# Hybrid RG-LRU and band-attention layer: x four steps apart, a PSUM bank for bounds, score slots and accumulators, late v places, gate columns, background counts

## The chip, the cores and the metric

The kernel runs on one core of one Trainium2 chip. The metric is the device time of one execution in microseconds. The engines are TensorE (PE, matmuls, with its weight loads as PEld), VectorE (DVE), ScalarE (ACT), GpSimd (POOL) and SyncE (SP), which only starts transfers. Each takes its instructions in order. PSUM, into which PE writes, has eight banks of 512 fp32 columns; DVE and ACT read it.

## What is computed

One layer of a streaming encoder, for a prompt of 2048 rows and a sample of 32 rows, width 1024, all in fp32:

```python
def layer_front(x, norm_g, w_in, q_g, k_g):
    z = rms_norm(x, norm_g) @ w_in
    xl, gl, q, k, v, ga = jnp.split(z, SPLITS, axis=-1)
    q = rms_norm(q.reshape(B, T, N_HEADS, HEAD_DIM), q_g)
    k = rms_norm(k.reshape(B, T, N_HEADS, HEAD_DIM), k_g)
...
xc, cbuf = causal_conv(xl, zeros, conv_w[l], conv_b[l])          # width 4
lru, h_last = rg_lru(xc, zeros, gate_a_w[l], gate_a_b[l], ...)   # scan over positions
att = band_attention_prompt(q, k, v, rel_bias[l])                # own 64-frame chunk and 8 before
...
def layer_back(x, lru, gl, att, ga, w_out, p, ple_g, w_pg, w_pe):
    mix = jnp.concatenate([lru * jax.nn.silu(gl), att * jax.nn.silu(ga)], axis=-1) @ w_out
    h = x + mix
    gate = jax.nn.sigmoid(rms_norm(h, ple_g) @ w_pg)
    return h + (p @ w_pe) * gate
```

It also returns the last 512 rows of k and v, the last convolution inputs and the LRU state. There are 8 heads of 64; the sample attends to 512 cached keys and its own 32.

## The kernel before

**Numbers.** PE multiplies fp16. Every fp32 operand is split into a high and a low fp16 half after scaling by a power of two from an absolute maximum; `products` issues three matmuls (hi·hi, hi·lo, lo·hi) for each 128 rows of the contraction. The split is `split`: the high half on POOL, ACT or DVE, the low half on DVE (L163). A maximum is spread over the partitions by `all_max`: DVE puts it on a diagonal (dg, L87), PE multiplies it by ones (psm, L90), DVE takes the maximum of the row (L91).

**Tiles.** The prompt is 16 tiles of 128 rows; a pair of tiles is a chunk (`c`, 8 of them) for the LRU. `load_x` and `prep_x` bring in a tile and normalise it: ACT's Square (L223), POOL's and DVE's split, and a transposing DMA into `xT[c][:, i % 2]`. x and xn have one buffer each, xT two (two chunks). `proj(i, b)` makes one of four blocks of 512 columns (1 k, 0 q, 2 v, 3 attention gate) of tile i in 24 matmuls (psp), and the `post_` functions finish it and store it in DRAM. `l_proj` makes the two LRU blocks in groups of 128 columns (psx, 48 matmuls of 256), `l_gates` the block-diagonal gates (psg at L641, read by ACT's sigmoids at L644 and L645), `l_tail` the scan, `l_halves` its halves.

**Order.** No planner: the generators `l_steps` (LRU of a chunk) and `background` (splitting w_out, w_ple_gate, w_ple_proj, the cache, and the bias rows into DRAM) are advanced by a few steps after each `proj` of the main loop, eight steps n = 0 to 7 per chunk. A scheduler then places the instructions on the engines' queues. `x_pair` says in which step of a chunk x is loaded and prepared. After the last chunk the late projections (v of tiles 12 to 15 and the attention gate) follow, without the pool of the early buffers.

**Attention.** A unit is one head of a tile (in tile 1 two heads): `u_scores` (pss, 10 matmuls into 640 columns in two banks), DVE adds the bias and takes the maximum (L988, for mx), ACT the exponential, `u_split` the halves and a transposing DMA (PT), `u_pv` five units later the product with v (pso, one bank for the 8 heads of a tile; `a_out` reads it at L1068 into att). Between the units `fill` advances the output side of the tile before: `o_out` (psu) and `o_gate` (psg and pse, from hT). At the end `fill` runs the sample's output among the last tile's: `prev` is tile 15's gate.

**PSUM before.** Projections: ps_p 3 banks, ps_x 3, ps_g 2 (gates and psm share them). Attention: ps_s two slots of two banks, ps_o 1, ps 3.

## Time and profile before

| what | us |
|---|---|
| median of three runs | 1235.5 (1233.63 to 1238.19) |
| the profiled execution | 1231.86 |
| its span | 1229.9 |
| PE busy in the span | 1078.4 (88%) |
| DVE busy | 850.8 (69%) |
| ACT busy | 591.3 (48%) |
| POOL busy | 430.5 (35%) |

The span is that of the profiled execution, from its first to its last instruction. Busy time says how long an engine worked, not that it was the one the others waited for. The stages lie one behind the other: start-up to 125 us, projections to about 650, the first units of attention to 725, steady attention to 1150, the tail.

### The profile page before, as it was taken

The page shows a single profiled execution, that of the slowest core. Times are in us where ns is not written, and L with a number is a line of the kernel's source. Part 1 is how long each engine was busy: PE and PEld are TensorE (multiplying, and loading weights), DVE is VectorE, ACT ScalarE, POOL GpSimd, SP SyncE. Part 2 cuts the span into 40 slices and gives each one's busy share as a digit, 9 for nine tenths or more (in the row PEclk, how much of TensorE's full clock was granted, in tenths as well). Part 3 has the DMA queues.
Part 4 walks back from the last instruction along what each step waited for, and adds up shares of the span by engine and source line. Part 5 has one row for each costly group of instructions (what it writes and reads, how often), then busy time and mean ns, then how long its engine had stood idle before and what let it go on. Part 6 is the DMA issues. An engine that isn't in the chain of part 4 may idle for free. (4 is left out here: it accounts for less than half of the span.)

```text
span 1229.9 us, 22389 instructions
## 1 busy us (share of the span) xinstructions
PE 1078.4 (88%) x8395; PEld 626.2 (51%) x8395; DVE 850.8 (69%) x1932; ACT 591.3 (48%) x1040; POOL 430.5 (35%) x482
## 2 busy tenths in 40 slices
PE   3779997997697988788988699999999999999896
PEld 1335664653364654565644355555555555555443
DVE  5997557666885676877855676677777777677544
ACT  6542374544636746247654344444445444545223
POOL 3875123444542437452421222222222222222221
PEclk9789998998898998899899699999999999999998
DMA  8785225994856476540498987999989998998841
GB/s 288 212 216 159 75 67 143 263 253 127 228 159 172 143 204 180 167 107 22 146 338 262 239 156 162 171 207 194 191 186 198 181 196 190 185 200 188 187 84 26
DMA packets 357725, 217.47 MB, mean 177 GB/s; under 512 B 296032, under 2 KB 298632, under 8 KB 357488
## 3 DMA queue, kind: packets, MB, share of 16 engines
q1 hardware_dynamic: 357184, 215.50, 72.0%
q8 instruction: 65, 1.06, 0.4%
q10 hardware_dynamic: 432, 0.54, 0.1%
q14 instruction: 44, 0.36, 0.1%
HBM read 98.87 MB, written 46.76 MB: 118 GB/s over the span
## 5 line engine op out<-in xcount | busy, mean ns | idle before, releaser
L183 PE MATMUL psp<-wA,xT 128*128 128x512 f16 x1536 | 368.3, 400 | 30.1 <-ACT sq L656 9.9
L183 PEld LDWEIGHTS <-xT 128*128 128x128 f16 x1536 | 155.9, 102 | 264.2 <-issue 82.0
L994 ACT ACTIVATE S<-S,nb,s 128x640 f32<-128x640 f32 (+5 forms) x130 | 110.5, 850 | 221.4 <-DVE nb L991 211.8
L183 PE MATMUL psg<-g,hT 128*128 128x512 f16 (+1 forms) x792 | 179.8, 376 | 4.4 <-DMA hT<-hn 2.7
L587 PE MATMUL psx<-xT,wl 128*128 128x256 f16 x1536 | 178.7, 276 | 0.0
L587 PEld LDWEIGHTS <-wl 128*128 128x128 f16 x1728 | 157.3, 99 | 25.6 <-issue 2.1
L1010 DVE TENSOR_TENSOR Phl<-S,Phl 128x640 f16<-128x640 f32 (+4 forms) x126 | 96.9, 773 | 89.4 <-POOL Phl L1007 52.7
L1032 PE MATMUL pso<-kv,PT 128*128 128x64 f16 (+1 forms) x1704 | 116.9, 195 | 25.6 <-DMA PT<-Phl 13.2
L1032 PEld LDWEIGHTS <-PT 128*128 128x128 f16 (+2 forms) x1800 | 109.7, 99 | 47.5 <-issue 16.8
L1007 POOL TENSOR_SCALAR Phl<-S 128x640 f16<-128x640 f32 (+4 forms) x63 | 49.1, 779 | 213.7 <-ACT S L994 179.8
L183 PEld LDWEIGHTS <-hT 128*128 128x128 f16 x792 | 73.6, 98 | 79.8 <-DMA hT<-hn 3.4
L977 PE MATMUL pss<-kv,qT 128*128 128x128 f16 (+2 forms) x1200 | 107.0, 221 | 6.3 <-DVE mx L988 4.4
L977 PEld LDWEIGHTS <-qT 128*128 128x128 f16 (+1 forms) x1200 | 93.9, 99 | 19.6 <-issue 6.2
L988 DVE CUSTOM_DVE_ANT_0 S<-pss,bias 128x640 f32<-128x640 f32 (+4 forms) x128 | 93.0, 731 | 2.5 <-PE pss L977 2.0
L183 PE MATMUL psu<-o,AT 128*128 128x512 f16 x384 | 91.8, 390 | 1.3 <-DMA AT<-An 1.3
L183 PE MATMUL psu<-o,L 128*128 128x512 f16 x384 | 88.0, 379 | 0.0
L1148 POOL TENSOR_TENSOR gt<-gt,h 128x512 f32<-128x512 f32 (+1 forms) x32 | 41.7, 1304 | 60.7 <-DVE gt L1147 56.4
L95 POOL TENSOR_SCALAR fh<-ssqh,e 128x8 f32<-128x8 f32 (+1 forms) x34 | 17.5, 514 | 126.4 <-DVE ssqh L282 99.8
L96 POOL TENSOR_TENSOR fh<-fh,pw 128x8 f32<-128x8 f32 (+1 forms) x34 | 61.0, 1793 | 1.6
L183 PEld LDWEIGHTS <-AT 128*128 128x128 f16 x384 | 36.6, 101 | 43.5 <-issue 5.7
L183 PEld LDWEIGHTS <-L 128*128 128x128 f16 x384 | 35.6, 98 | 38.5
L90 PE MATMUL psm<-dg,ones 128*128 128x128 bf16 x25 | 6.0, 241 | 55.7 <-DVE dg L87 29.7
(284 smaller groups left out, 1693.5 us busy)
## 6 DMA issues: line engine op xcount, KB each, us to landing
stw<-in_w_in_dram SPq DMA_DIRECT2D x20, 512.0 KB, 7.1
x<-in_x_prompt_dram SPq DMA_DIRECT2D x16, 512.0 KB, 4.8
stg<-in_w_out_dram SPq DMA_DIRECT2D x16, 512.0 KB, 5.1
stg<-in_w_ple_gate_dram SPq DMA_DIRECT2D x16, 512.0 KB, 4.8
qT<-qd SPq DMA_DIRECT2D x32, 256.0 KB, 5.4
kv<-kvd SPq DMA_DIRECT2D x16, 512.0 KB, 4.1
h<-in_x_prompt_dram SPq DMA_DIRECT2D x16, 512.0 KB, 4.5
out_dram<-gt SPq DMA_DIRECT2D x31, 256.0 KB, 2.3
```

The lines of the kernel that those rows point to most:

```text
L90: nc.tensor.matmul(ps, lhsT=ones, rhs=dg, start=True, stop=True)
L95: nc.gpsimd.tensor_scalar(dst, ssq, mul, add, op0=OP.mult, op1=OP.add)
L96: nc.gpsimd.tensor_tensor(dst, dst, pw[:R, :n], op=OP.pow)
L183: m = nc.tensor.matmul(ps[:R], lhsT=l(a), rhs=r(e), start=first and j == 0, stop=last and j == 2)
L587: m = nc.tensor.matmul(o, lhsT=wl[j][:, k, a, g * 128:(g + 1) * 128], rhs=rhs, start=i == 0, stop=i == 23)
L977: last_mm[0] = nc.tensor.matmul(ps[rw, c], lhsT=q[:, h % 2, a * 4 + h // 2, :R], rhs=k[:, h, :n], start=a == 0, stop=a == 1)
L988: nc.vector.tensor_tensor_reduce(out=S[:, c0:c0 + W], in0=ps[:, c0:c0 + W], in1=bias[:, h, 640 - W:], op0=OP.add, op1=OP.max, scale=1.0, s ...
L994: nc.scalar.activation(S[:, c0:c0 + W], S[:, c0:c0 + W], AF.Exp, bias=nb[:, j:j + 1], scale=scP, accum_out=sums[i][:, e:e + 1])
L1007: nc.gpsimd.tensor_scalar(v[:, 0, :W], P[:, :W], 1.0, 1.0, op0=OP.mult, op1=OP.mult)
L1010: nc.vector.tensor_tensor(v[:, 1, :W], P[:, :W], v[:, 0, :W], op=OP.subtract)
L1032: nc.tensor.matmul(o[rw, o0:o0 + HD], lhsT=t[:n, a * (WP // 128) + c0 // 128 + j, rw], rhs=v[:n, e, h * HD:h * HD + HD], start=first and m ...
L1148: (nc.vector if end else nc.gpsimd).tensor_tensor(gt[:R], gt[:R], s["h"][:R, c], op=OP.add)
```

## The change

- `psm` gets a pool of its own with one bank (ps_m); ps_x has two banks instead of three; ps_g serves the gates alone.
- `x_pair` is called with the current chunk: in step 1 the second tile of this chunk is prepared and the first of the next loaded, in step 5 that one is prepared and the next loaded. The sample's x comes in chunk 2 (SP - 1). `load_x(4)`, `prep_x(4)` and `load_x(5)` move forward, into the first chunks.
- The background steps after each of the eight steps of a chunk are 3, 4, 5, 5, 4, 4, 4, 1 instead of 3, 4, 4, 4, 3, 4, 4, 4: 30 either way.
- Tiles 13 and 15 keep v (vTo and vo) in places of their own in a pool that is opened when the early buffers are closed.
- The scores have one PSUM tile of three banks with two slots, columns 0 to 639 and 896 to 1535 for a full unit; the second slot does its first key block last. ps_o gets two banks.
- At the end four steps of `prev` instead of two come before the sample's gate: the first 512 columns and 256 of tile 15's gate, 768 in all.

```diff
@@ -85,7 +85,7 @@
         floor2(p2, src)
         dg = sm.tile([128, 128], BF16, tag="dg", name="dg", bufs=1)
         nc.vector.tensor_scalar(dg, ident, p2, None, op0=OP.mult)
-        ps = ps_g.tile([128, 2, CW], F32, tag="g", name="psm").rearrange("p a b -> p (a b)")[:, :128]
+        ps = ps_m.tile([128, 128], F32, tag="m", name="psm")
         with tc.issue_after(after.ins) if after else nullcontext():
             nc.tensor.matmul(ps, lhsT=ones, rhs=dg, start=True, stop=True)
         nc.vector.tensor_reduce(dst, ps, axis=AX.X, op=OP.max)
@@ -198,8 +198,9 @@
     lc = pool("lc", stack=esl)
     st0 = pool("st0", stack=es0)
     ps_p = pool("ps_p", bufs=3, space=PSUM, stack=esr, side="right")
-    ps_x = pool("ps_x", bufs=3, space=PSUM, stack=esl)
+    ps_x = pool("ps_x", bufs=2, space=PSUM, stack=esl)
     ps_g = pool("ps_g", bufs=2, space=PSUM, stack=esl)
+    ps_m = pool("ps_m", bufs=1, space=PSUM, stack=esl)
     absmax(gmax[:, 0:1], col[:, G:G + 8])
     absmax(gmax[:, 1:2], col[:, PG:PG + 8])
     for j in range(2):
@@ -317,11 +318,12 @@
 
     def post_v(i):
         R, ps = rows(i), pj.pop((i, 2))
-        t = Tp("vTo", [128, 2, 512], F16, 1)
+        late = i in (NT - 3, NT - 1)
+        t = T("vTo", [128, 2, 512], F16, 1, pv2) if late else Tp("vTo", [128, 2, 512], F16, 1)
         nc.scalar.activation(t[:R, 0], ps[:R], AF.Copy, scale=2.0 ** -20)
         nc.vector.scalar_tensor_tensor(t[:R, 1], ps[:R], 2.0 ** -20, t[:R, 0], op0=OP.mult, op1=OP.subtract)
         if i == SAMPLE or i >= NT - 4:
-            vo = Tp("t512", [128, 512], F32, 2)
+            vo = T("vo", [128, 512], F32, 1, pv2) if late else Tp("t512", [128, 512], F32, 2)
             nc.scalar.activation(vo[:R], ps[:R], AF.Copy, scale=u_v[:R])
             nc.sync.dma_start(out_sv if i == SAMPLE else out_pv[(i - NT + 4) * 128:(i - NT + 5) * 128, :], vo[:R])
         nc.sync.dma_start(kv_d[i][:R, 1], t[:R].rearrange("p a b -> p (a b)"))
@@ -777,6 +779,7 @@
     proj(3, 1)
     with tc.issue_after(last_w.ins):
         lru_factors()
+    load_x(4)
     es_lt = es0.pop_all()
     proj(3, 0)
     prep_w_in(3, stg[3])
@@ -787,6 +790,9 @@
         next(ls)
         proj(i, b)
         next(ls)
+        if (i, b) == (2, 3):
+            prep_x(4)
+            load_x(5)
         for _ in range(4):
             next(bg)
     lp = None
@@ -795,17 +801,18 @@
     def x_pair(n, c):
 
         if n == 1:
-            load_x(2 * c)
-        elif n == 4:
-            prep_x(2 * c)
-            load_x(2 * c + 1)
-        elif n == 6:
             prep_x(2 * c + 1)
-
-    load_x(4)
-    prep_x(4)
-    load_x(5)
-    prep_x(5)
+            load_x(2 * c + 2)
+        elif n == 5:
+            prep_x(2 * c + 2)
+            load_x(SAMPLE if c == SP - 1 else 2 * c + 3)
+        elif n == 7 and c == SP - 1:
+            prep_x(SAMPLE)
+            load_x(2 * c + 3)
+        elif n == 7 and c == NCH - 3:
+            prep_x(2 * c + 3)
+            load_x(2 * c + 4)
+
     lss = l_steps(SAMPLE)
     for c in range(2, NCH - 2):
         steps = [(i, b) for i in (2 * c, 2 * c + 1) for b in (1, 0, 2, 3)]
@@ -817,17 +824,14 @@
             next(lp, None)
             if c == 2:
                 next(lp, None)
-            for _ in range(4 if n % 4 else 3):
+            for _ in range((3, 4, 5, 5, 4, 4, 4, 1)[n]):
                 next(bg, None)
             if c == SP and n % 2:
                 proj(SAMPLE, (1, 0, 2, 3)[n // 2])
             if c == SP + 1:
                 next(lss, None)
                 next(lss, None)
-            x_pair(n, c + 1)
-            if c == SP - 1 and n == 7:
-                load_x(SAMPLE)
-                prep_x(SAMPLE)
+            x_pair(n, c)
     c = NCH - 2
 
     def dense(lp, ls, steps):
@@ -844,7 +848,6 @@
         pass
     for _ in lss:
         pass
-    load_x(2 * c + 2)
     prep_x(2 * c + 2)
     load_x(2 * c + 3)
     prep_x(2 * c + 3)
@@ -874,6 +877,7 @@
         return t
 
     esp.close()
+    pv2 = pool("pv2", stack=esr, side="right")
     for i in range(12, 16):
         proj(i, 2)
     proj(12, 3)
@@ -889,8 +893,10 @@
     ch = pool("ch")
     ao = pool("ao")
     ol = pool("ol")
-    ps_s = pool("ps_s", bufs=2, space=PSUM)
-    ps_o = pool("ps_o", bufs=1, space=PSUM)
+    ps_s = pool("ps_s", bufs=1, space=PSUM)
+    ps_o = pool("ps_o", bufs=2, space=PSUM)
+
+    ps3, nss = ps_s.tile([128, 1536], F32, name="ps3"), [0]
     units, acc, sums = {}, {}, {}
     kv, qT, sgT, nkv = {}, {}, {}, [0]
 
@@ -965,11 +971,15 @@
     def u_scores(i, u):
 
         ks = keys_of(i)
-        ps = ps_s.tile([128, 640], F32, tag="s", name="pss")
         q = qT[i]
         parts, W, WP = unit_parts(i, u)
+        second, nss[0] = nss[0] % 2, nss[0] + 1
+        ps = ps3[:, 1536 - WP:] if second else ps3[:, :WP]
+        blocks = list(enumerate(ks))
+        if second:
+            blocks = blocks[1:] + blocks[:1]
         for together in [parts] if i == SAMPLE else [[p] for p in parts]:
-            for j, (key, n) in enumerate(ks):
+            for j, (key, n) in blocks:
                 k = k_of(key)
                 for a in range(2):
                     for h, R, rw, c0 in together:
@@ -1158,7 +1168,7 @@
             o = o_out(i)
             if i == SAMPLE:
 
-                for g, k in ((o, 4), (prev, 2), (o_gate(i), 4), (o, 1), (prev, 9)):
+                for g, k in ((o, 4), (prev, 4), (o_gate(i), 4), (o, 1), (prev, 9)):
                     for _ in range(k):
                         if next(g, 0) != 0:
                             yield
```

How the change moves instructions is shown at three places. A name in square brackets is the semaphore of the engine waited for.

PE's queue in the projections, before: a psm (L90) behind four gate matmuls (psg) and ahead of a projection of the sample (xT_s). It waits for ACT.

```order
L641 LDWEIGHTS gw
L641 MATMUL psg<-X,gw 128x256
L641 LDWEIGHTS gwl
L641 MATMUL psg<-X,gwl 128x256
L90 LDWEIGHTS ones [waits DVE_49,PE_49]
L90 MATMUL psm<-dg,ones 128x128 [waits Activation_49]
L181 LDWEIGHTS xT_s
L181 MATMUL psp<-wA_232,xT_s 32x512
```

After, the same psm: it stands behind the gates before, ahead of 48 psx matmuls.

```order
L643 LDWEIGHTS gwl
L643 MATMUL psg<-X,gwl 128x256
L90 LDWEIGHTS ones
L90 MATMUL psm<-dg,ones 128x128 [waits DVE_49]
L589 LDWEIGHTS wl_238
L589 MATMUL psx<-xT,wl_238 128x256 [waits Activation_49]
```

It moved forward by 48 psx, 24 psp and 4 psg matmuls, no longer waits for ACT, and waits for DVE (dg).

DVE's queue at the tail of chunk 2, before: from the maximum of the chunk before (mbL) to the first instruction of `l_tail` (L652). hlA are halves of the background, hl those of the LRU.

```order
L91 TENSOR_REDUCE mbL<-psm 128x1 [waits PE_49]
L680 RECIPROCAL ms<-mbL 128x1 [waits DVE_49]
L308 TENSOR_TENSOR t_2962<-t_2951,fh 32x512 [waits DMAHW6_49,Pool_49]
L681 TENSOR_SCALAR ms<-ms 128x1 [waits DVE_49]
L163 SCALAR_TENSOR_TENSOR hlA<-stg,sg,hlA 128x512 [waits DMAHW6_49,Pool_49]
L163 SCALAR_TENSOR_TENSOR hlA<-stg,sg,hlA 128x512 [waits DMAHW7_49,Pool_49]
L282 TENSOR_REDUCE ssqh<-t_2996 128x8 [waits Activation_49]
L163 SCALAR_TENSOR_TENSOR hl<-sl_1640,ms,hl 128x512 [waits Pool_49] x2
L163 SCALAR_TENSOR_TENSOR hlA<-stg,sg,hlA 128x512 [waits DMAHW1_49,DMAHW3_49,DVE_49,Pool_49]
L652 TENSOR_TENSOR r_2781<-r_2781,cl 128x1024 [waits Activation_49]
```

After, the same stretch; L652 is now L654.

```order
L91 TENSOR_REDUCE mbL<-psm 128x1 [waits PE_49]
L682 RECIPROCAL ms<-mbL 128x1 [waits DVE_49]
L683 TENSOR_SCALAR ms<-ms 128x1 [waits DVE_49]
L309 TENSOR_TENSOR t_2975<-t_2964,fh 32x512 [waits Pool_49]
L163 SCALAR_TENSOR_TENSOR hl<-sl_1634,ms,hl 128x512 [waits Pool_49] x2
L283 TENSOR_REDUCE ssqh<-t_3009 128x8 [waits Activation_49]
L292 TENSOR_TENSOR t_3016<-psp,fh 128x512 [waits DVE_49,Pool_49]
L654 TENSOR_TENSOR r_2784<-r_2784,cl 128x1024 [waits Activation_49]
```

The three hlA rows are gone from the stretch; they stand earlier in the queue.

PE's queue in steady attention, before: the start of a unit behind the 12 products of `o_out` (psu). Score matmuls (pss) and products with v (pso) alternate.

```order
L183 LDWEIGHTS AT
L183 MATMUL psu<-o_6846,AT 128x512
L977 LDWEIGHTS qT
L977 MATMUL pss<-kv,qT 128x128 [waits DVE_49]
L1032 LDWEIGHTS PT [waits DMAHW0_49]
L1032 MATMUL pso<-kv,PT 128x64
L977 LDWEIGHTS qT
L977 MATMUL pss<-kv,qT 128x128
```

After, a unit of the same kind: the score tile is ps_6833, and L977 is now L987.

```order
L1042 LDWEIGHTS PT
L1042 MATMUL pso<-kv,PT 128x64
L987 LDWEIGHTS qT
L987 MATMUL ps_6833<-kv,qT 128x128 [waits DVE_49]
L987 LDWEIGHTS qT
L987 MATMUL ps_6833<-kv,qT 128x128
```

The ten score matmuls stand together behind eleven or more products with v; the first of them waits for DVE. In the program this wait is for the read of the unit just before; in the kernel before it is for the read of the unit two before.

## Rows read from the trace of the kernel before

**Rows 1.** Busy time by stretch of the span, core 0: the stretch, its length, then the busy time of each engine (instructions in brackets), TensorE's granted clock, the share of DMA time and GB/s.

```profile
200.00:500.00 300.00, 251.02 (x1681) 145.89 (x1679) 208.21 (x412) 161.47 (x279) 133.55 (x140) 0.92 0.70 194
...
650.00:725.00 75.00, 55.33 (x442) 31.40 (x441) 49.01 (x161) 33.22 (x80) 16.72 (x23) 0.86 0.93 233
725.00:1150.00 425.00, 408.96 (x3930) 238.34 (x3928) 295.63 (x706) 194.88 (x341) 116.49 (x142) 0.99 0.92 186
```

**Rows 2.** What the TensorE queue waited for over the whole span: engine, tile and line that waited, engine, tile and line waited for; us in total, times, the longest in us.

```profile
PE psm L90 <- DVE dg L87: 29.7, 5, 11.9
PE psm L90 <- ACT ig L645: 22.3, 6, 7.7
...
PE pso L1032 <- DVE att L1068: 12.4, 12, 2.2
PE psp L183 <- ACT sq L656: 9.9, 1, 9.9
...
PE psg L181 <- DMA hT<-hn: 5.2, 1, 5.2
PE psp L183 <- ACT t L325: 4.8, 1, 4.8
PE pss L977 <- DVE mx L988: 4.4, 6, 1.7
```

**Rows 3.** What ScalarE waited for from 200 to 500 us, columns as in rows 2.

```profile
ACT xn L223 <- DMA xT<-xn: 23.2, 4, 9.7
ACT xn L223 <- DMA x<-in_x_prompt_dram: 20.8, 4, 7.6
...
ACT xn L223 <- DMA x<-in_x_sample_dram: 6.0, 1, 6.0
```

**Rows 4.** Timeline of ScalarE and TensorE near 290 us: start, length (both us), engine, line, operation, output and input, shapes, how many in one, and in brackets the idle time just before and what ended it.

```profile
288.86 1.06 ACT L223 ACTIVATE xn<-x 128x1024 f16<-128x1024 f32 x1 [9.71 <-DMA xT<-xn]
...
290.48 0.55 ACT L644 ACTIVATE r<-psg,col,ug 64x256 f32<-64x256 f32 x1
...
286.73 0.27 PE L641 MATMUL psg<-X,gwl 128*128 128x256 f16 x1
292.80 0.27 PE L90 MATMUL psm<-dg,ones 128*128 128x128 bf16 x1 [5.80 <-ACT ig L645]
```

**Rows 5.** Timeline of TensorE and VectorE from 262 to 274 us, columns as in rows 4.

```profile
262.27 5.40 PE L587 MATMUL psx<-xT,wl 128*128 128x256 f16 x48
268.51 5.35 PE L183 MATMUL psp<-wA,xT 128*128 128x512 f16 x24 [0.83 <-DVE m L135]
...
270.25 0.23 DVE L87 TENSOR_SCALAR dg<-ident,p 128x128 bf16<-128x128 bf16 x1
```

**Rows 6.** Timeline of TensorE from 201 to 217 us, columns as in rows 4.

```profile
201.74 0.38 PE L183 MATMUL psp<-wA,xT 128*128 128x512 f16 x1
209.85 0.26 PE L90 MATMUL psm<-dg,ones 128*128 128x128 bf16 x1 [7.74 <-ACT ig L645]
209.91 6.31 PE L183 MATMUL psp<-wA,xT 128*128 128x512 f16 x15
```

**Rows 7.** Timeline of TensorE from 484 to 503 us, columns as in rows 4.

```profile
484.85 5.40 PE L587 MATMUL psx<-xT,wl 128*128 128x256 f16 x48
...
502.57 0.27 PE L90 MATMUL psm<-dg,ones 128*128 128x128 bf16 x1 [6.16 <-DVE dg L87]
```

**Rows 8.** Steady attention: one tile's stretch (columns as in rows 1), what VectorE waited for from 800 to 1130 us (as in rows 2), and four of its reads of scores (as in rows 4).

```profile
998.10:1030.61 32.51, 31.44 (x310) 18.53 (x309) 22.96 (x57) 14.83 (x28) 9.12 (x11) 1.00 0.95 194
...
DVE Phl L1010 <- POOL Phl L1007: 38.6, 20, 2.1
DVE Phl L1010 <- ACT Phl L1009: 28.9, 31, 1.9
...
986.59 0.82 DVE L988 CUSTOM_DVE_ANT_0 S<-pss,bias 128x640 f32<-128x640 f32 x1
988.24 0.81 DVE L988 CUSTOM_DVE_ANT_0 S<-pss,bias 128x640 f32<-128x640 f32 x1
...
994.34 0.82 DVE L988 CUSTOM_DVE_ANT_0 S<-pss,bias 128x640 f32<-128x640 f32 x1
...
998.07 0.82 DVE L988 CUSTOM_DVE_ANT_0 S<-pss,bias 128x640 f32<-128x640 f32 x1
```

**Rows 9.** Timeline of VectorE, ScalarE and TensorE at the tail of a chunk, 309 to 319 us, columns as in rows 4.

```profile
309.87 2.33 DVE L163 SCALAR_TENSOR_TENSOR hlA<-stg,sg,hlA 128x512 f16<-128x512 f32 x1 [1.79 <-POOL hlA L158]
...
313.38 1.06 ACT L653 ACTIVATE th<-r 128x1024 f32<-128x1024 f32 x1 [5.50 <-DVE r L652]
...
318.40 3.89 PE L183 MATMUL psp<-wA,xT 128*128 128x512 f16 x10 [9.86 <-ACT sq L656]
```

**Rows 10.** Timeline of ScalarE and TensorE near 643 us, columns as in rows 4.

```profile
643.02 0.69 ACT L325 ACTIVATE t<-psp,u 128x512 f32<-128x512 f32 x1 [1.99 <-DVE vTo L322]
...
643.75 6.54 PE L183 MATMUL psp<-wA,xT 128*128 128x512 f16 x17 [4.85 <-ACT t L325]
```

**Rows 11.** Timeline of TensorE from 1210 to 1221 us, columns as in rows 4.

```profile
1210.19 3.60 PE L181 MATMUL psg<-g,hT 128*32 128x512 f16 x24 [5.24 <-DMA hT<-hn]
...
1214.42 2.62 PE L181 MATMUL psg<-g,hT 128*32 128x512 f16 x24
...
1217.41 2.79 PE L183 MATMUL psg<-g,hT 128*128 128x256 f16 x24
```

## The prediction

> **What bounds the kernel now.** I began with the stages. Read the first columns of [rows 1]: from 725 to 1150 us (attention) TensorE (PE) is busy 408.96 of 425 us at a granted clock of 0.99, so little is left there; from 200 to 500 us (the input projections) it is busy 251.02 of 300 at 0.92, and from 650 to 725 us 55.33 of 75 at 0.86. What can be won lies in the projections. The list of PE's waits [rows 2] names them: psm (the one matmul that spreads a maximum over the partitions) for ScalarE (ACT) 22.3 us in 6 times, one stop of 9.9 us for ACT's sq, one of 4.8 us for ACT's t at L325, one of 5.2 us in the tail, and 12 of about 1 us in attention (pso for att).
>
> Removing a PE wait pays only if PE is what the others wait for. In the projections it is not. ACT itself stands still there: 23.2 us at L223 (the Square of prep_x) for the transposing DMA of the x tile before, 26.8 us for loads of x [rows 3]. [Rows 4] shows how that reaches PE: the Square at 288.86 came after 9.71 us of idleness, the gate sigmoids stood behind it in ACT's queue, and PE's psm, which wanted the bank they read, started at 292.80 after 5.80 us. In attention the vector side sets the pace too: one tile takes 32.51 us for 31.44 of PE, VectorE (DVE) never waits for PE between 800 and 1130 us, but 38.6 and 28.9 us for the fp16 halves made by GpSimd (POOL) and ACT [rows 8]. So I count a removed PE wait at less than its length, and ask each time what comes next.
>
> **The change, part by part**, against the profiled execution's 1231.86 us; the median of three runs is 1235.5, that is 3.6 more, which I add at the end. Gains are positive.
>
> Own bank for psm. At 201.74 PE stopped 7.74 us and the 15 products after it took 6.31 us, 421 ns each, against 5.35/24 = 223 ns elsewhere [rows 5, 6]. With a bank of its own psm passes, PE does the next 24 products (5.35 us) and then stops at the next gates, whose bank ACT empties no earlier. Between 0 and 7.7; I take 2.5, because the group after that again needs a place that the vector side frees. The 5.80 us at 286.73 goes in the same way, but the Square stays ahead of the sigmoids, as it waits for the same transposing DMA in both orders: 0 to 5.8, I take 1.5. The remaining psm stops of the 22.3 us: 1. Together +5.
>
> Moved psm. Freed from its bank, psm is also placed earlier: the first one shown in the order stands ahead of 48 psx products instead of behind them and 24 more. PE reached that place at 262.27, but DVE made its dg at 270.25 [rows 5]: a new stop of up to 8.2 us, with 48 products queued behind it, and ACT and DVE waiting for those. PE gives part of it back, since it waited 0.83 us and more soon afterwards anyway. The psm that stopped 6.16 us until 502.57 now stands ahead of the 48 products begun at 484.85 [rows 7]; with dg at its old time this is 17.5 us of stop, 11.4 more, but DVE now makes dg 17 rows earlier. Bounds 0 and -20; I take -5.
>
> Background counts. At 308.4 PE stopped 9.86 us for a slot that ACT had to empty; ACT had waited 5.50 us for DVE's L652, which stood behind background splits (hlA), one of them 2.33 us after 1.79 us of waiting for POOL [rows 9]. In the new order no hlA stands between the maximum (mbL) and L652; before there were three. The number of background steps in all is the same, so they fall due in the middle of a chunk instead, where POOL and DVE also have work. Bounds 0 and 9.9 at this chunk, I take 4, and 1.5 at each of two later chunk tails: +7.
>
> x four steps apart. The pair's second Square still waits for the transposing DMA of the first, and that one for PE's last psx on the buffer of the chunk before; this chain is in both orders, so the 23.2 us stay. The x loads (26.8 us of ACT) get a step or so more, on an SP queue that carries the background's stores in order. Bounds -3 and +10; I take +1.
>
> Two ps_x banks instead of three. PE never waits for ps_x in the list of waits. The nearest row is another pool with two places, pss for mx: 4.4 us in 6 times, 0.7 each [rows 2]. With some two tight pairs per chunk this is 0 to -4; I take -1.5.
>
> Late v places. PE's 4.85 us stop ended with ACT's L325 at 643.02, and the 17 products after it took 6.54 us, 2.75 more than 17 times 223 ns [rows 10, 5]. With own places for v of tiles 13 and 15 both can go: 7.6. But tile 15's copy still waits for tile 13's store. Bounds 0 and 7.6; I take 5.
>
> Scores and accumulators. In the order the first matmul of each unit's scores now waits for DVE's read of the unit just before; it used to be the unit two before. So the two slots work as one. Does PE get there in time? A tile's 31.44 us are 8 units, six of about 3.6 and two of 4.9 us (six products more). DVE read scores at 986.59, 988.24, 994.34 and 998.07, for 0.82 us each [rows 8]. PE may start the unit read at 988.24 when the read before it ends, 987.41, needs some 0.6 us, and is just in time. The next starts after 3.6 to 4.9 us, by 992.3, and is wanted at 994.34; the next by 995.9, wanted at 998.07. The lead shrinks from several us to 0.2 at the tightest read but holds, so the period of 32.5 us stays; PE's stop for att goes, and gives nothing, as it was not the pacer. I take -2 over 12 tiles and -1 for 650 to 725 us, where the first units are uneven. Bounds +4 and -15. The Trainium skill, PSUM — Partial Sum Buffer, section on bank collisions, says that engines must not touch one bank at the same time; that would make only the blocks in the middle bank wait, 2 matmuls of 10, and this term would be 0. The order puts the wait on the first matmul, and I go by the order.
>
> 768 gate columns first. The sample's gate stopped PE 5.24 us for hT, and its first 24 products took 3.60 us, the next 24 of the same form 2.62. 256 columns of tile 15 (24 products, 2.79 us, and 6 more [rows 11]) now fill most of that stop. Less work stands behind the sample, but the last DVE and DMA steps after PE's end stay. Bounds 0 and 5; I take +3.
>
> Sum: 5 - 5 + 7 + 1 - 1.5 + 5 - 3 + 3 = 11.5. 1231.86 - 11.5 = 1220.4, and with 3.6 for the median **1224**.
>
> **The rivals.**
> *The shorter chain.* If the spacing of x does take ACT's load waits and the counts clear every tail, their upper bounds (10 and 9.9 + 3) stand in place of 1 and 7: 15 us more, 1224 - 15 = 1209. For it speaks that ACT's 50 us at L223 are the largest idleness of the stage; against it that the transposing DMAs keep their place.
> *Every PE wait counts.* 22.3 + 9.9 + 4.8 + 5.2 + 12.4 = 54.6 of [rows 2], less the 5, 1.5 and 3 lost: 45, so 1190. Against it speak ACT's idleness [rows 3] and DVE's [rows 8], which are not PE's doing. The Trainium skill, Perfetto Trace Analysis, section Identifying the Most-Contended Engine, would have one go for the busiest engine first, and its section Optimization Strategy for the gaps on it; this rival is that rule.
> *No change.* The vector engines take back all that PE gains in the projections, and attention loses 3: late v 5, tail 3, less 1.5, 3 and 2 of new stops leave 1.5: 1234.
> *Slower through the scores.* With one slot PE cannot work ahead: each uneven DVE gap becomes PE idleness that no later unit repays. Price: 0.25 us in each of 8 units of 12 tiles is 24 us, 1224 + 21 = 1245. It decides from about 1.4 us per tile, where it has eaten the 11.5 and the 6 of the bound. For it: the tightest read has 0.2 us to spare. Against: the next gap of 6.1 us repays.
> *Slower through the moved psm.* Its bound of -20 in place of -5: 1239.
>
> **How the numbers follow.** Forecast (1217 to 1231) 0.38, shorter chain 0.20, every wait 0.04, no change 0.18, slower by scores 0.12, by psm 0.08. A measurement of this kernel tells 0.5% from no change, 6.2 us: faster means below 1229.3. Faster: four fifths of the forecast and both larger gains, 0.54; within: 0.24; slower: 0.22. The range 1206 to 1244 leaves out the every-wait case, the lower part of the shorter chain and the upper part of the scores.
>
> **What would show it.** Right: psm for ACT ig gone from PE's waits, with psm for DVE dg larger; no stop near 308 of over 6 us; the one for L325 gone; tile period 32.5 +- 0.4 with pss for mx as PE's main wait in attention. Wrong: ACT's L223 waits down from 50 us to under 25 (shorter chain), or a period above 33.5 (scores). DVE rows that wait for pss would show that the slot, not the vector loop, sets the pace.

## The result, and the profile after

The changed kernel takes 1241.97 us, median of 7 runs (1240.36 to 1246.95), against 1234.21 us (1231.61 to 1238.19, 7 runs) for the kernel before. The ratio is 1.0057, 95% interval 1.0036 to 1.0078: slower by about 0.6%, a little more than this measurement can tell from no change. 1224 was predicted, with 1206 to 1244 as the range and 0.22 for slower: the sign was wrong. The profiled execution of the kernel after took 1246.6 us (span 1244.9), 14.7 more than that of before; it is one of the longer ones, so its differences are read here for their place and their cause, and the medians for their size.

The stretches of [rows 1] and the steady tile of [rows 8], in the profile after (columns as there):

```profile
200.00:500.00 300.00, 258.67 (x1712) 150.31 (x1711) 210.84 (x422) 161.08 (x281) 129.80 (x140) 0.92 0.74 199
650.00:725.00 75.00, 51.27 (x364) 27.64 (x364) 39.05 (x135) 26.91 (x65) 12.01 (x19) 0.77 0.81 214
725.00:1150.00 425.00, 405.30 (x3878) 237.06 (x3878) 304.54 (x719) 197.50 (x348) 116.56 (x141) 0.99 0.94 185
976.64:1009.11 32.47, 31.44 (x310) 18.61 (x309) 23.89 (x57) 15.43 (x27) 9.01 (x12) 1.00 1.00 197
```

The projections (200 to 500 us) hold 31 more TensorE instructions than before and TensorE (PE) is busier. A steady tile of attention takes 32.47 us, as before. What stands out is the short stretch between them: from 650 to 725 us PE carries out 364 matmuls where it carried out 442, all five busy times are lower, and the granted clock is 0.77 where it was 0.86. That is where the time went.

What PE waited for in the whole span, after (columns as in [rows 2]):

```profile
PE psm L90 <- DVE dg L87: 46.8, 8, 11.4
PE ps L987 <- DVE mx L998: 27.2, 19, 5.9
...
PE psg L643 <- ACT ig L647: 12.8, 4, 5.3
...
PE psg L181 <- DMA hT<-hn: 3.0, 1, 3.0
```

Of [rows 2], psm for ScalarE (ACT), the stop of 9.9 us for sq, the one for t at L325 and pso for att are gone, as forecast. In their place psm waits 46.8 us for VectorE's (DVE) dg instead of 29.7, the gates wait 12.8 us for ig instead of 7.8, and the scores wait for DVE's mx 27.2 us in 19 times instead of 4.4 in 6.

To see where time was lost rather than where PE stood, I set the same instruction of two traces side by side: the start of DVE's n-th read of scores (L988 before, L998 after; 128 reads, the first eight of tile 0, the next eight of tile 1, and so on), minus its start in the kernel named in the last line of the heading.

| read | after | slots_only | one_slot | no_slots | rest_first_slots | rest_gate_slots |
|---|---|---|---|---|---|---|
| against | before | before | before | before | rest_first | rest_gate |
| 0 | -1.6 | -1.8 | -2.0 | -0.9 | +4.2 | +1.6 |
| 3 | +6.1 | +5.1 | +4.2 | -6.1 | +11.4 | +5.7 |
| 6 | +12.3 | +11.7 | +11.0 | -1.2 | +8.8 | +1.6 |
| 15 | +14.9 | +14.2 | +13.5 | -1.4 | +9.4 | +3.8 |
| 16 | +6.1 | +5.2 | +4.7 | -3.6 | +11.7 | +5.3 |
| 27 | +20.5 | +19.5 | +19.3 | -3.5 | +24.3 | +10.5 |
| 32 | +16.1 | +16.3 | +16.2 | -3.3 | +19.3 | +4.4 |
| 48 | +15.1 | +14.8 | +14.6 | -3.9 | +16.7 | +11.2 |
| 90 | +14.1 | +15.0 | +14.5 | -3.6 | +14.0 | +33.0 |
| 126 | +16.0 | +15.0 | +14.5 | -4.2 | +13.3 | +57.7 |

The first column is the finding: attention begins 1.6 us early and is 15 us late by read 15, the last of tile 1. At read 16 only 6 us are left, by read 27 (tile 3) it is 20 us late, and from there to the end the lag swings between 12 and 21 us and ends near 15. So the time is lost in tiles 0 to 3, and not in the steady tiles behind them. (The other columns belong to the experiments.)

A lag at one read is not all lost time, since the scheduler also places other products differently between the reads. The scores of read 15 stand behind 24 products of the output side (psu, some 5 us) in the kernel after, and ahead of them in the kernel before, which pauses for 13.9 us between its reads 15 and 16; at read 16 as many products stand ahead in both. At read 27 it is 32 more in the kernel after. At equal work, then, the loss is some 6 us at the end of tile 1 and some 13 us in tile 3 (estimates, with 5.34/24 us a product).

The same place in PE's timeline, before (start, length, what, and in brackets the idle time just before):

```profile
651.70 0.28 PE L977 MATMUL pss<-kv,qT 128*128 128x128 f16 x2
652.25 0.27 PE L977 MATMUL pss<-kv,qT 128*128 128x128 f16 x2 [0.27 <-DVE mbL L91]
652.36 5.34 PE L183 MATMUL psp<-wA,xT 128*128 128x512 f16 x24
657.53 0.39 PE L977 MATMUL pss<-kv,qT 128*128 128x128 f16 x4
657.81 5.34 PE L183 MATMUL psp<-wA,xT 128*128 128x512 f16 x24
...
670.21 0.39 PE L977 MATMUL pss<-kv,qT 128*128 128x128 f16 x4
670.43 0.66 PE L1032 MATMUL pso<-kv,PT 128*128 128x64 f16 x9
```

And after:

```profile
643.77 0.28 PE L987 MATMUL ps<-kv,qT 128*128 128x128 f16 x2
649.52 0.27 PE L90 MATMUL psm<-dg,ones 128*128 128x128 bf16 x1 [5.47 <-DVE dg L87]
655.72 0.37 PE L987 MATMUL ps<-kv,qT 128*128 128x128 f16 x2 [5.94 <-DVE mx L998]
655.89 7.69 PE L183 MATMUL psp<-wA,xT 128*128 128x512 f16 x24
663.41 0.28 PE L987 MATMUL ps<-kv,qT 128*128 128x128 f16 x2
670.12 0.34 PE L1042 MATMUL pso<-kv,PT 128*128 128x64 f16 x3 [6.43 <-DMA PT<-Phl]
670.28 0.40 PE L987 MATMUL ps<-kv,qT 128*128 128x128 f16 x2
670.47 7.23 PE L183 MATMUL psp<-wA,xT 128*128 128x512 f16 x24
677.54 0.28 PE L987 MATMUL ps<-kv,qT 128*128 128x128 f16 x2
```

DVE's first read, before and then after, and its fourth after:

```profile
656.96 0.28 DVE L988 CUSTOM_DVE_ANT_0 S<-pss,bias 128x128 f32<-128x128 f32 x1
```

```profile
655.37 0.29 DVE L998 CUSTOM_DVE_ANT_0 S<-ps,bias 128x128 f32<-128x128 f32 x1
...
670.72 0.29 DVE L998 CUSTOM_DVE_ANT_0 S<-ps,bias 128x128 f32<-128x128 f32 x1 [5.83 <-PE ps L987]
```

In tile 0 a unit is one head, two score matmuls. Before, PE hands over the first two units (651.70 and 652.25) and goes on into 24 projection products while DVE has read neither. After, the second unit's first matmul waits for the read of the first, which DVE reaches hardly earlier than before (655.37 against 656.96), and PE stands still for 5.94 us with the 24 products queued behind it. A second stop, 6.43 us, is for the transposing DMA (PT): the first unit's product with v (pso) now stands ahead of the fourth unit's scores, where before the first pso stands behind all eight units of the tile. The one slot has changed the built order there; one_slot, below, has the same two stops (5.42 and 4.72 us). After each stop the products also take longer: 7.69 and 7.23 us for the 24 that take 5.34. The stops and the slower products come to 16.6 us (some stops of before are gone). DVE in turn stands still for PE. Its waits for scores from 638 to 760 us, before and then after:

```profile
DVE S L988 <- PE pss L977: 2.0, 1, 2.0
```

```profile
DVE S L998 <- PE ps L987: 22.3, 10, 5.8
```

PE waits for DVE and for the DMA, and DVE for PE, in turns, much more than before. The list of PE's waits alone (13.0 us in 7 times for mx in this stretch) would not have told which of the two is late.

In tiles 2 and 3 there are no projections left; there the products between the units are those of the output side. Ahead of the units 21 to 27 (numbered as the reads) the trace of before has 22, 0, 2, 0, 19, 0 and 5 of them, the trace of after 21, 3, 14, 10, 0, 19 and 13: units that PE handed over in pairs mostly come one by one.

### The profile page after: what moved, and what is told of

Same layout as the page of the kernel before. It is cut to its first block, busy times and chain, and to the rows that moved or that the text cites. A ratio compares the mean times of both kernels' runs of the same rounds, so it can differ in the third digit from the quotient of the medians.

```text
span 1244.9 us, 22337 instructions
## 1 busy us (share of the span) xinstructions
PE 1082.6 (87%) x8395; PEld 627.7 (50%) x8395; DVE 858.4 (69%) x1932; ACT 589.5 (47%) x1038; POOL 424.4 (34%) x482
## 5 line engine op out<-in xcount | busy, mean ns | idle before, releaser
L987 PE MATMUL ps<-kv,qT 128*128 128x128 f16 (+2 forms) x1200 | 86.0, 221 | 31.1 <-DVE mx L998 27.2
L998 DVE CUSTOM_DVE_ANT_0 S<-ps,bias 128x640 f32<-128x640 f32 (+4 forms) x128 | 93.1, 729 | 26.9 <-PE ps L987 22.3
L1017 POOL TENSOR_SCALAR Phl<-S 128x640 f16<-128x640 f32 (+4 forms) x63 | 42.6, 676 | 178.2 <-ACT S L1004 162.5
L1042 PEld LDWEIGHTS <-PT 128*128 128x128 f16 (+2 forms) x1800 | 75.1, 99 | 43.4 <-DMA PT<-Phl 18.3
L1042 PE MATMUL pso<-kv,PT 128*128 128x64 f16 (+1 forms) x1704 | 85.3, 195 | 13.0 <-DMA PT<-Phl 12.9
L987 PEld LDWEIGHTS <-qT 128*128 128x128 f16 (+1 forms) x1200 | 69.5, 99 | 45.4 <-issue 41.1
L183 PE MATMUL psu<-o,L 128*128 128x512 f16 x384 | 90.8, 384 | 0.0
L1122 DVE SCALAR_TENSOR_TENSOR h<-psu,cA,h 128x512 f32<-128x512 f32 x64 | 47.4, 740 | 16.4 <-PE psu L183 16.4
```

The costliest lines, as they stand in the source:

```text
L183: m = nc.tensor.matmul(ps[:R], lhsT=l(a), rhs=r(e), start=first and j == 0, stop=last and j == 2)
L987: last_mm[0] = nc.tensor.matmul(ps[rw, c], lhsT=q[:, h % 2, a * 4 + h // 2, :R], rhs=k[:, h, :n], start=a == 0, stop=a == 1)
L998: nc.vector.tensor_tensor_reduce(out=S[:, c0:c0 + W], in0=ps[:, c0:c0 + W], in1=bias[:, h, 640 - W:], op0=OP.add, op1=OP.max, scale=1.0, s ...
L1017: nc.gpsimd.tensor_scalar(v[:, 0, :W], P[:, :W], 1.0, 1.0, op0=OP.mult, op1=OP.mult)
L1042: nc.tensor.matmul(o[rw, o0:o0 + HD], lhsT=t[:n, a * (WP // 128) + c0 // 128 + j, rw], rhs=v[:n, e, h * HD:h * HD + HD], start=first and m ...
L1122: nc.vector.scalar_tensor_tensor(h[:R, c], pt[:R], cA[:R, j, half:half + 1], h[:R, c], op0=OP.mult, op1=OP.add)
```

## Experiments

Each kernel was timed beside the kernel before on the same chip; ratios are to it, with the 95% interval. Differences in us are such a ratio times the median of before on that chip, 1230.7 to 1232.3 us here.

**The change in parts.** no_slots is the change without the part on scores and accumulators, slots_only that part alone:

```diff
-    ps_s = pool("ps_s", bufs=2, space=PSUM)
-    ps_o = pool("ps_o", bufs=1, space=PSUM)
+    ps_s = pool("ps_s", bufs=1, space=PSUM)
+    ps_o = pool("ps_o", bufs=2, space=PSUM)
+    ps3, nss = ps_s.tile([128, 1536], F32, name="ps3"), [0]
...
+        second, nss[0] = nss[0] % 2, nss[0] + 1
+        ps = ps3[:, 1536 - WP:] if second else ps3[:, :WP]
...
```

> The changed kernel with its scores and accumulators as before (two slots of two banks, one accumulator bank). Theory A, the score slots cost at the start of attention (PE reached the last projection 13.3 us later than in the kernel before, after being level at 638 us) and the rest of the change gains a little: 1226 to 1231, faster than before, and PE's waits for DVE mx fall from 27.2 us back to about 4. Theory B, the loss comes from the moved psm and the new order of the projections: 1238 to 1242, as slow as the changed kernel.

> The kernel before with only the three-bank score tile and the two accumulator banks. Theory A: 1243 to 1249, slower by 9 to 15 us, with PE waiting over 20 us for DVE mx, half of it before 760 us. Theory B: 1233 to 1236, no difference.

Measured: no_slots 0.9963 (0.9944 to 0.9981), slots_only 1.0139 (1.0117 to 1.0162). This one part costs 17 us (14 to 20) and the rest of the change gains 4.6 (2.3 to 6.9). In the table above slots_only follows the whole change from read to read, and no_slots loses nothing.

end_only has the late v places and the 768 gate columns; proj_only has psm's own bank with two ps_x banks, the spacing of x and the background counts.

> The kernel before with only the late v places and the 768 gate columns first. Theory A: 1226 to 1230; the 4.8 us stop for ACT at L325 is gone and the 5.2 us stop for hT is 3 us or less. Theory B says the same of the end but expects no more than 3 us: 1231 to 1234, since the first units of attention wait for the vector side anyway.

> The kernel before with only the own bank for psm, two ps_x banks, the spacing of x and the background counts. Theory A: 1232 to 1237, no difference, because the lead that PE wins is given back at the next wait for DVE (level at 638 us). Theory B: 1238 to 1244, slower by the new stops of psm for dg (46.8 us in 8 times against 29.7 in 5).

Measured: end_only 0.9976 (0.9959 to 0.9992), proj_only 1.0011 (0.9992 to 1.003). The four projection edits together are worth nothing that can be measured.

**Is it one slot, or the accumulators?** one_slot is the kernel before with a single, ordinary score tile and two accumulator banks; one_slot_one_acc has the single score tile alone (without the lines on ps_o).

```diff
-    ps_s = pool("ps_s", bufs=2, space=PSUM)
-    ps_o = pool("ps_o", bufs=1, space=PSUM)
+    ps_s = pool("ps_s", bufs=1, space=PSUM)
+    ps_o = pool("ps_o", bufs=2, space=PSUM)
```

> The kernel before with one score slot of two banks instead of two slots, and two accumulator banks. If the two slots of the three-bank tile work as one, this takes the same time as the kernel with the score part of the change alone (1.0139 of the kernel before): 1244 to 1252. If the second slot of the three-bank tile is still worth something, this is slower than that by 5 us or more.

> The kernel before with one score slot of two banks and nothing else; the accumulator keeps its one bank. If the second accumulator bank gives nothing, since the vector engines set the pace of a tile: within 3 us of the kernel with one slot and two accumulators. If it gives back PE's stop of about 1 us per tile: slower than that one by 8 to 15 us.

Measured: 1.0142 (1.012 to 1.0164) and 1.0154 (1.0134 to 1.0173). A true single slot costs what the two slots in one tile cost, read for read (table above), and PE waits for its scores as there:

```profile
PE pss L977 <- DVE mx L988: 24.2, 20, 5.4
```

So the two slots do work as one, and the second accumulator bank gives nothing that can be told (the intervals overlap).

**The two edits at the end.** tail_only has the 768 columns, late_only the places for v of tiles 13 and 15 (in the diff one line of each, in this order; late_only also opens the pool and places vo).

```diff
-                for g, k in ((o, 4), (prev, 2), (o_gate(i), 4), (o, 1), (prev, 9)):
+                for g, k in ((o, 4), (prev, 4), (o_gate(i), 4), (o, 1), (prev, 9)):
...
+        late = i in (NT - 3, NT - 1)
+        t = T("vTo", [128, 2, 512], F16, 1, pv2) if late else Tp("vTo", [128, 2, 512], F16, 1)
```

> The kernel before with only the 768 gate columns first. If the gain of the end comes from here and not from the late v places: 1227 to 1230, the same as with both. If the late v places carry it: 1231 to 1234.

> The kernel before with only the late v places. If PE's lead of 8 us at tile 13 is given back at the first units of attention: 1231 to 1235, no difference, with the stop for ACT at L325 gone and larger stops for PT and mx soon after. If the lead is kept: 1225 to 1229.

Measured: tail_only 0.9966 (0.9946 to 0.9986), a gain of 4.2 us; late_only 1.0032 (1.0012 to 1.0051), a loss of 3.9. In the tail, PE's stop for hT of [rows 11] shrank from 5.24 to 1.93 us, and the 24 products behind it from 3.60 to 1.91:

```profile
1213.94 1.91 PE L181 MATMUL psg<-g,hT 128*32 128x512 f16 x24 [1.93 <-DMA hT<-hn]
```

In late_only the stop for t is gone [rows 10], and this is what came instead, in PE's timeline:

```profile
646.78 0.26 PE L90 MATMUL psm<-dg,ones 128*128 128x128 bf16 x1 [5.92 <-DVE dg L87]
646.88 0.38 PE L979 MATMUL pss<-kv,qT 128*128 128x128 f16 x2
648.05 0.37 PE L979 MATMUL pss<-kv,qT 128*128 128x128 f16 x2 [0.79 <-DVE mbL L91]
...
657.49 0.48 PE L979 MATMUL pss<-kv,qT 128*128 128x128 f16 x4 [2.34 <-DVE mx L990]
```

PE reached psm early, but its dg was no earlier; then it waited for the read of the scores. A projection group whose last product started 10.9 us ahead of before (3.2 of them already won one group earlier) was followed, two groups later, by one that was 1.7 us behind. That does not explain the loss, though: in this trace DVE's reads 16 to 115 start 2 to 5 us ahead of before, they are level at the end, and the execution (1231.15 us) is no longer than that of before.

Nor is the sign settled. The late places can be taken from three pairs of kernels: alone they lose 3.9 us (1.5 to 6.3), from tail_only to end_only 1.2, and from proj_tail (below) to no_slots they gain 3.3; the 1.2 lie within the intervals, the 3.3 barely outside them.

**The projection edits one by one.** bank_only has psm's own bank and two ps_x banks, bg_only the background counts, x_only the spacing of x; the diff has a line of each in this order, and the rest of x_only is the moved loads of the change's diff.

```diff
-        ps = ps_g.tile([128, 2, CW], F32, tag="g", name="psm").rearrange("p a b -> p (a b)")[:, :128]
+        ps = ps_m.tile([128, 128], F32, tag="m", name="psm")
...
-            for _ in range(4 if n % 4 else 3):
+            for _ in range((3, 4, 5, 5, 4, 4, 4, 1)[n]):
...
-            x_pair(n, c + 1)
+            x_pair(n, c)
```

> The kernel before with only the own bank for psm and two ps_x banks. If the vector side sets the pace of the projections, the 7.7 us and the other stops of psm for ACT go and come back as other waits: 0.997 to 1.003 of the kernel before, level within 3 us at the last projection. If the own bank were worth its removed stops: 0.985 or less.

> The kernel before with only the background counts. By the prediction, which gave this part 7 us: 0.994. By the other reading, that the background steps only move and take the same time of POOL and DVE in the middle of the chunk: 0.998 to 1.002; the stop of 9.9 us near 308 us becomes smaller and others grow.

> The kernel before with only the spacing of x. By the prediction, 1 us: 0.998 to 1.002, with ACT's wait at the Square for the transposing DMA still over 20 us. If the spacing does what its name says, that wait is halved and the ratio 0.992 or less.

Measured: bank_only 0.9992 (0.9974 to 1.0009), bg_only 1.0035 (1.002 to 1.0049), x_only 1.0022 (1.0005 to 1.0038). PE's waits for dg in bank_only, then in bg_only, and others of bank_only:

```profile
PE psm L90 <- DVE dg L87: 31.1, 7, 11.6
```

```profile
PE psm L90 <- DVE dg L87: 45.1, 7, 11.5
```

```profile
PE psg L642 <- ACT ig L646: 9.1, 3, 5.2
...
PE psp L183 <- DVE vTo L323: 6.6, 2, 3.9
PE psp L183 <- DVE ga L341: 5.8, 2, 5.1
PE psp L183 <- DVE t L292: 5.2, 1, 5.2
```

Two things follow. The bank takes away the 22.3 us for ig and moves the end by 1.0 us (-1.1 to 3.2): the last product of a projection group started 10.9 us ahead of before at 207 us, and three groups later 0.5 us behind. And the moved psm, which the prediction put down to the bank, comes with the background counts: 31.1 us of dg with the bank alone (29.7 before), 45.1 with the counts alone, one of them 8.32 us at 269.32, where bank_only has none. The counts do take away the stop of 9.86 us of [rows 9]; what PE gains there it pays at psm. In x_only, ACT still waits for x tiles from 200 to 500 us as in [rows 3]:

```profile
ACT xn L223 <- DMA x<-in_x_prompt_dram: 30.3, 5, 11.0
ACT xn L223 <- DMA xT<-xn: 23.6, 4, 10.0
```

**Do the parts add up?** proj_tail is proj_only with the 768 columns, bank_tail is bank_only with them (both edits as above).

> The changed kernel without the score slots, the accumulators and the late v places: what is left if both parts that cost time are taken out. If the parts add up (tail 0.9966, projections 1.001): 0.995 to 0.999. If the late v places cost only beside the old order of the projections: the same as without the slots alone, 0.9963.

> The kernel before with the two parts that cost nothing when taken alone: the own bank for psm and the 768 gate columns first. If the parts add up (0.9992 and 0.9966): 0.994 to 0.998, 1224 to 1229, faster than both kernels. If the lead of the one is eaten by the next wait: 0.998 to 1.001.

Measured: proj_tail 0.999 (0.9973 to 1.0008), bank_tail 0.9968 (0.9951 to 0.9985). The bank adds nothing to the tail, and the x spacing and the counts seem to take some of its gain away (the intervals overlap). Sums of parts miss by up to 0.45%, more than the intervals: no_slots and slots_only add up to 1.0102, and the whole change is 1.0057. By the difference of the whole change and no_slots the score part costs 12 us (8 to 15) and not 17. Where that lies stays open.

**Is it the projections between the scores?** rest_first is the kernel before with its last three projections called ahead of attention; rest_first_slots has the score part as well. Both, and the two kernels after them, also load w_out's second set of weights (o1) ahead of attention.

```diff
-    rest = [(13, 3), (14, 3), (15, 3)]
+    rest = []
+    for p in ((13, 3), (14, 3), (15, 3)):
+        proj(*p)
```

> The kernel before with its three last projections put ahead of the attention units instead of between them. A reference for the next run: between 1225 and 1245; PE then does 16 us of projections with nothing beside them, but the units are no longer cut up.

> The same with the score part of the change. If the one slot costs its 15 us because 24 projection matmuls stand in PE's queue between two scores and DVE waits behind them, it costs 5 us or less here against the run without it. If it costs them through the short units of the first tiles as such, it costs 12 us or more here too.

Measured: rest_first 1.0007 (0.999 to 1.0023), rest_first_slots 1.0088 (1.0058 to 1.0118). One slot costs 10 us here (6 to 14) and not 17, which is in neither expected band. The edit did not do what I meant it to: in PE's timeline the first unit's scores (640.47) and the second's (670.42) still have 96 projection products between them, since the second waits for a read and the order that is built goes on with products meanwhile.

So I tied the scores of the first eight units behind the last product of these projections (issue_after sets a block's instructions behind the one named on its engine), without (rest_gate) and with the score part (rest_gate_slots).

```diff
+    rest_mm = last_mm[0]
...
-        u_scores(i, u)
+        with tc.issue_after(rest_mm.ins) if n < 8 else nullcontext():
+            u_scores(i, u)
```

> The kernel before with the three last projections ahead of the units, and with the score matmuls of the first eight units tied behind the last product of these projections, so that no projection stands between scores on PE. Computes all of the reference. It is the base for the next run. Theory (what one slot costs comes from the 24-product projections that stand between the first scores): against the kernel before 0.997 to 1.010, since the first scores start later, some 10 us of projections behind one another. Rival (short units cost by themselves): the same.

> The same with the scores in one PSUM tile of two slots and two accumulator banks. Computes all of the reference. Theory (projections between scores make the loss): at most 5 us more than the run above, and VectorE's waits for score matmuls from 640 to 760 us within 6 us of those of the run above. Rival (one slot costs short units by themselves, whatever stands between them): 10 us or more above the run above, as without the tie.

Measured: rest_gate 1.0096 (1.0066 to 1.0127), rest_gate_slots 1.0514 (1.048 to 1.0548). By the total the rival's band is met five times over, but the table shows that two things lie in it. Up to read 32 one slot loses about 4 us (3.8 at read 15, 4.3 at read 24, 4.4 at read 32, with swings up to 13 between), where with projections between the scores it lost 13.5 to 14.2 at read 15 and 16.2 to 16.3 at read 32. DVE's waits for scores from 640 to 760 us are 6.2 against 2.9 us, 3.3 more, within the 6 that the theory allowed. Later, from read 48 on, it goes on losing, in steady attention, where the change itself loses nothing. DVE's waits there, 800 to 1150 us, in rest_gate_slots (slots_only has none for scores):

```profile
DVE S L997 <- PE ps L986: 37.8, 35, 2.9
```

The built order differs there. In slots_only each of 16 successive units from read 96 on has 12 or 18 products of other tiles (psu, psg, pse) ahead of its scores; in rest_gate_slots they number 22, 20, 22, 14, 0, 23, 19, 21, 23, 21, 1 and then five times 0. PE's timeline shows a heavy one:

```profile
1035.61 0.72 PE L986 MATMUL ps<-kv,qT 128*128 128x128 f16 x10
1036.17 0.86 PE L1041 MATMUL pso<-kv,PT 128*128 128x64 f16 x24
1036.87 2.11 PE L183 MATMUL psu<-o,L 128*128 128x512 f16 x9
1038.81 2.97 PE L183 MATMUL psg<-g,hT 128*128 128x512 f16 x13
1041.62 0.72 PE L986 MATMUL ps<-kv,qT 128*128 128x128 f16 x10
```

The start of one unit's scores lies 6.01 us (1035.61 to 1041.62) ahead of the next one's there, where a steady tile has eight units in 32.5 us, 4.1 each.

What follows: the loss of the first tiles comes from the work that stands between their scores; with the projections ahead of the units it is 4.4 us at read 32, where it was 16. How it divides between the wait for the read, the pso that waits for PT and the slower products behind a stop, no run separates. It isn't to be had back by moving that work ahead, though: with two slots rest_gate alone costs 12 us (8 to 16), and its sixteenth read is 11.5 us later than before (691.3 against 679.8). A second slot is what lets scores and projections overlap, and a single one gives that up. The later loss of rest_gate_slots stands beside an uneven filling; that the filling is its cause is likely but not shown, since no run changed it alone.

## Why the prediction was wrong

**The step that failed** is the term "Scores and accumulators", -2 over 12 tiles and -1 for 650 to 725 us. Its mechanism was right: the first matmul of a unit waits for the read just before, the two slots work as one (slots_only against one_slot), and steady attention keeps its period (32.47 us) because the read comes in time. What was mis-sized is the -1 for the first units: it measured about -15 in the traces, -17 in the ratio of slots_only, and -12 as the difference of the whole change and no_slots. I had worked out PE's lead over DVE for a unit of 3.6 to 4.9 us and gave the uneven first units a token. There the question has another answer, as groups of 12 to 24 products stand between the scores. With two slots PE goes into such a group with two units unread; with one it stands in front of the second unit until DVE has read the first, 5.94 us at the start, and the built order then runs into PT for 6.43 us more. The rows for it were in the trace of before (x4 score matmuls between groups of 24), and I had not looked at them. Of the term's bounds, -15 was the right end.

At the end of tile 1 half of the lag is gone again, in a pause of the kernel before. What is left from tile 4 on isn't repaid: PE is busy 405.30 of the 425 us from 725 us on, with little room to catch up. This also tells why the rival "slower through the scores" gave nearly the right time (1245) from the wrong place: it asked for 0.25 us in each unit of 12 steady tiles, and the change lost nothing there. DVE's waits for scores in steady attention exist in rest_gate_slots, but beside an uneven filling that the built order of the change does not have. That the measured time lies inside the stated range is luck too: the score term alone used up its bound, and the other terms came to little, with both signs.

The signs named for a right forecast all came: psm for ig gone and dg larger, no stop over 6 us near 308 (4.21 at 314.36; the one that the prediction puts at 308.4 began at 308.54), the stop at L325 gone, the steady tile at 32.47 us, and mx as PE's main wait from 725 to 1150 us (17.7 us in 14 times). They tested the mechanisms and not their prices. The last sign named, DVE waiting for scores, did come, in the first tiles alone: 22.3 us from 638 to 760, none from 800 to 1130.

**Late v places** (+5): the stop went, and 3.9 us were lost (1.5 to 6.3) in late_only, where other pairs of kernels give a loss of 1.2 and a gain of 3.3. The lead of PE met dg and then the first reads, both DVE's. I had priced the stop and not asked who was next, though the text named that question. Whether the places gain or lose stays open.

**Background counts** (+7) and **moved psm** (-5): the counts alone lost 4.3 us (2.5 to 6.0). The stop at the tail of the chunk did shrink, and the new stop at 272.41 us came longer than its bound of 8.2 us:

```profile
263.47 0.27 PE L643 MATMUL psg<-X,gwl 128*128 128x256 f16 x1
272.41 0.27 PE L90 MATMUL psm<-dg,ones 128*128 128x128 bf16 x1 [8.66 <-DVE dg L87]
272.46 8.27 PE L589 MATMUL psx<-xT,wl 128*128 128x256 f16 x48
```

The 48 products behind it took 8.27 us where they had taken 5.40 [rows 5]. The two were one edit's two sides, and I had taken the gain at three chunk tails and the loss at a fourth of its bound. The second moved psm, priced at up to 11.4 us, starts at 485.55 us in the profile after with no wait ahead of it: its dg came earlier too.

**Own bank** (+5) and **two ps_x banks** (-1.5): together 1.0 us (-1.1 to 3.2). The stops for ig went. Little of them came back as the gates' own wait for ig, which the prediction expected one group later (9.1 us in bank_only, 7.8 before). More came back as waits for DVE at the projections: 6.6 us for vTo (2.5 before), 5.8 for ga (0.8) and 5.2 for t at L292 (none). The prediction gave the removal 5 us, and it was worth less.

**x four steps apart** (+1): -2.7 us (-0.6 to -4.7) alone. The transposing waits stayed, as forecast, and ACT's waits for x in the whole change are hardly shorter, 48.8 us together against 50.0:

```profile
ACT xn L224 <- DMA xT<-xn: 29.8, 4, 12.7
ACT xn L224 <- DMA x<-in_x_prompt_dram: 19.0, 3, 11.0
```

**768 gate columns** (+3): 4.2 us (1.7 to 6.6), right in mechanism and size.

**The sum.** The projection terms came to +6.5 and measured -1.4 (-3.7 to 1.0, proj_only): in the whole change the last product of the group ahead of the stop of [rows 10] starts at 638.4 us, and before at 638.5. The end terms came to +8 and measured +3.0; the score term -3 and -17 (-12 within the whole change). The argument that a removed PE wait counts for less than its length was right, and I did not follow it far enough: in the projections it counts for nothing here. The rival "every PE wait counts" (1190) fell with that: the 22.3 us taken from PE's gaps in bank_only moved the end by 1. The prediction took this rival for the rule of the Trainium skill, Perfetto Trace Analysis, Identifying the Most-Contended Engine, with PE as the busiest engine. The page itself does not judge TensorE by its matmul time but by its matmul rate and the busy share of its weight loads. These loads were busy 145.89 of the 300 us of the projections, and DVE 208.21 [rows 1], so the rule as it stands there does not plainly point at PE, and the runs do not speak against it. The other page the prediction weighed, the Trainium skill, PSUM — Partial Sum Buffer, on bank collisions, says that engines must not access one bank at the same time; that only the blocks in the shared middle bank would wait was worked out from it. The traces speak for a wait of the whole tile: the first of the ten matmuls waits, and slots_only and one_slot agree to 0.0003.

A version that beats both kernels: the kernel before with the 768 gate columns alone (tail_only, 0.9966, 0.9946 to 0.9986), one line. no_slots (0.9963) and bank_tail (0.9968) are no better within the intervals.

## What to carry to other kernels

A buffer is not judged by the steady state alone: ask at the first units, where other work stands between its users, how many units the producer can hand over before it goes into that work, and how long that work is. Where slots share one tile, look in the built order for which read the first write waits before counting them as two. And a stop of an engine that doesn't set the pace is worth nothing until the trace names the engine that does and shows that it gets its input earlier; otherwise the time is given back at the next stops, in bank_only within three groups of products.

## What was not expected of the hardware

A PE stop costs more than its length, since the products after it run slower. I had read single rows of this [rows 6], but not counted it into any stop of the change: 24 products took 7.69 us after a stop of 5.94, and 48 took 8.27 after 8.66, where 5.34 and 5.40 are the times elsewhere. The granted clock goes with it (columns as in [rows 1]). The 24 products after the stop, in the profile after, with the stop ahead of them:

```profile
649.79:655.72 5.93, 0.00 (x0) 0.00 (x0) 3.41 (x9) 2.02 (x3) 1.36 (x2) 0.50 1.03 409
655.90:663.58 7.68, 7.68 (x28) 3.01 (x26) 1.11 (x6) 2.48 (x6) 0.30 (x1) 0.69 0.79 292
```

And 24 products without a stop, before:

```profile
657.81:663.15 5.34, 5.34 (x28) 2.50 (x26) 1.96 (x7) 4.42 (x7) 0.00 (x0) 1.00 0.97 313
```

In the stop the clock is at 0.50, the lower level of 1.2 GHz, and the products behind it run a part of their time at that level. From 650 to 725 us, with several such stops, it was 0.77 (0.86 before). A lost overlap is paid for in waiting, and again in the clock behind it.
